# A hybrid decoder block: output projection by column halves, pooling and gate evacuated by ScalarE, first MLP sums on GpSimd

## The chip, the cores and the metric

The kernel runs on one core of a Trainium2 chip. The metric is the device time of one execution in microseconds (us). Three runs of the kernel before took 1162.57 to 1164.47 us, median 1163.44. In the profile PE is TensorE (matmul), DVE is VectorE, ACT is ScalarE, POOL is GpSimd and SP is SyncE, which issues most DMAs here.

## The reference

One decoder layer over a sequence of 1024 tokens with 1024 channels, all in float32:

```
h    = rms_norm(x, norm1_g)
proj = h @ w_in           # 8 heads x 64: q, k, v | 8 gate logits | conv input 512 | pool input 256
att  = forgetting attention: q, k normalised per head, causal, with the running sum of
       log_sigmoid(gate + b_f) as a bias, in blocks of 128 queries
conv = GLU -> causal depthwise conv of width 31 -> LayerNorm -> SiLU -> 256x256 matmul
pool = (trailing mean over 2, 4, 8, 16 tokens - self) -> 64x64 matmul per group -> scale
x    = x + concat(att, conv, pool) @ w_out          # 1024 -> 1024
h2   = rms_norm(x, norm2_g)
up   = causal depthwise conv of width 3 over h2 @ w_up     # 1024 -> 2 x 2816
out  = x + (silu(gate half of up) * value half of up) @ w_down
```

## The kernel before

**Arithmetic.** Every large product is made of three matmuls in a fast 32-bit format: each operand is split into a rounded high part and a low part (`split`, L47 to L49: ACT casts the high part, DVE or, where `lo` says so, POOL subtracts it from the source), and `mm3` (L51 to L55) issues high x high (L53), high x low (L54) and low x high (L55). A weight is ready for L53 when ACT has cast it and for L54 or L55 when the low part is there too.

**Order of the work.** The code is written for a tile framework. Its build-time scheduler puts the instructions of each engine in one fixed order and inserts the waits; each engine then runs its queue strictly in that order, so one instruction that waits holds up all behind it. The code says what depends on what, and, by generators that are advanced with `step` or `next`, what is offered to the scheduler early.

**Stage 1, to about 233 us: input projection.** x and `w_in` are loaded; eight 128-row pieces of x, transposed, are the operands `hh` and `hl` (k = 0 to 7). `feat_mm` makes the convolution and pooling inputs with channels on partitions, in two halves of 512 tokens. `feat_evac` takes each result from PSUM, times the token's 1/rms (`rb`): for kind "b" into `u` and through a sigmoid, for kind "a" into `ar` and on POOL times `u`, and in the branch under `else` into `pu`. That branch belongs to the test for "a" alone, so kind "b" runs it too and writes values into `pu` that the kind "p" overwrites later: eight products in all, L190. Then `values_in` makes v in token tiles of 128 (256 columns, in the second call 264, of which 8 are the gate logits: ACT evacuates v, DVE the gates, L422), and `heads_in` q and k. Weights come through `load_two` (two k at a time) and `load_wide` (one k, 512 columns), over two buffers named `wr`; a `wr` is free when both halves have been read.

Beside this runs the generator `side_work`: the 31 taps of the convolution over two channel groups and two halves (124 operations of 128x512 on DVE, L262 and L266, one accumulator `acc` each), and between the two channel groups the pooling chain `pool_work`: shifted adds `pn` (L234), the window's mean minus self into `d` (L245), a corrected first 16 columns copied into `d` (L247), the split of `d` into `dhl`, and a product `tp` on PE, evacuated into `mcp` (L254). After the values, `gate_cumsum` (L364 on) turns the gate logits `fgt` into log-sigmoids `fz` by ACT's Exp and Ln with DVE steps between, and sums them along the tokens.

**Stage 2, to about 430 us: attention.** 32 stages, eight heads times four blocks of 256 queries: `scores` (PE `s`, ACT exponential, DVE and POOL for the split), transposes `t`, `values`. Into these stages a second generator, `fill`, puts tiles of the output projection that need only the convolution and pooling half of the input: one tile is 12 matmuls into a bank `f`, for token tile t and one half of the output columns (L611 to L624). `mix_work` does tokens 0 to 511 for column half 0, waits until the last q and k are prepared (`prep_done`, from stage 23), then does the other three parts. A fill is offered from stage 4 on in every second stage, and in every stage once `prep_done` is set. The sums are kept in four tiles `x2`, each with two token tiles over all columns.

**Stage 3, to about 510 us.** `mix_att` adds the attention half of the output projection (banks `c`) to `x2`. `h2T` (L731 to L762) writes a token tile to DRAM by a DMA that POOL issues, takes its sum of squares on ACT and 1/rms on POOL (`ss`), scales it on DVE (`xh`, L738), transposes it on PE (`d`) and splits it into the four quadrants that the MLP needs. The MLP is a seven-product (Strassen) scheme; of the first block of `w_up`, `add_sums(0)` makes the four sums `ws` of quadrants on DVE (L712 to L719), called after token tile 3.

**Stage 4 and 5, to the end:** 22 blocks of the up-projection with the width-3 convolution and the gate, then the down-projection. The diff touches neither.

Of the kernel before, what the change touches and what calls it, by code (L numbers as in the profile page):

```python
# [16 lines left out]
P = 128  # L17
# [4 lines left out]
H = 8  # L22
# [17 lines left out]
def tile_hybrid_block(ctx: ExitStack, tc: tile.TileContext, x: bass.AP, xT: bass.AP, prm: bass.AP,  # L40
# [6 lines left out]
    def split(dst_hi, dst_lo, src, lo=None):  # L47
        nc.scalar.copy(out=dst_hi, in_=src)  # L48
        (lo or nc.vector).tensor_tensor(out=dst_lo, in0=src, in1=dst_hi.bitcast(F32), op=ALU.subtract)  # L49
# [62 lines left out]
    def tpps():  # L112
        return ptp.tile([P, 512], F32, name="tp", tag="tp")
# [63 lines left out]
    def feat_evac(pss, f, half):  # L177
        kind, i = f
        sl = slice(half * 512, half * 512 + 512)
        if kind == "b":  # L180
            ub = u[:, i, PAD + half * 512:PAD + half * 512 + 512]
            nc.vector.tensor_tensor(out=ub, in0=pss, in1=rb[:, sl], op=ALU.mult)
            nc.scalar.activation(out=ub, in_=ub, func=AF.Sigmoid)
        if kind == "a":
            ua = u[:, i, PAD + half * 512:PAD + half * 512 + 512]
            ar = raw((P, 512), "ar")
            nc.vector.tensor_tensor(out=ar, in0=pss, in1=rb[:, sl], op=ALU.mult)
            nc.gpsimd.tensor_tensor(out=ua, in0=ar, in1=ua, op=ALU.mult)
        else:
            nc.vector.tensor_tensor(out=pu[i][:, 16 + half * 512:528 + half * 512], in0=pss, in1=rb[:, sl],  # L190
                                    op=ALU.mult)

# [22 lines left out]
    def pool_work():  # L215
# [10 lines left out]
        for i in range(2):  # L226
# [22 lines left out]
            for half in range(2):  # L249
                dhl = sp.tile([P, 2, 512], F32R, name="dhl", tag="shl")  # L250
                split(dhl[:, 0], dhl[:, 1], d[:, half * 512:half * 512 + 512])
                ps = tpps()
                mm3(ps, pw_hl[:, 0, i, :], pw_hl[:, 1, i, :], dhl[:, 0], dhl[:, 1], True, True)
                nc.vector.tensor_scalar(out=mcp[half][:, 2 + i, :], in0=ps, scalar1=pc(PC_PS + i), scalar2=None,  # L254
                                        op0=ALU.mult)
                yield
# [107 lines left out]
    def gate_cumsum():  # L364
        fz = sp.tile([P, NT * H], F32, name="fz", bufs=1)
        z = fgt.rearrange("p t h -> p (t h)")
        nc.vector.scalar_tensor_tensor(out=fz, in0=z, scalar=-1.0, in1=z, op0=ALU.mult, op1=ALU.max)
# [45 lines left out]
    def values_in(c0, w, n, then, steps):  # L413
        for t in range(NT):
# [6 lines left out]
            if w > 256:  # L421
                nc.vector.scalar_tensor_tensor(out=fgt[:, t, :], in0=ps[:, 256:264], scalar=rstd[:, t:t + 1],  # L422
                                               in1=par[:, PC_BF:PC_BF + H], op0=ALU.mult, op1=ALU.add)
            step(steps)
# [44 lines left out]
    for k in range(4, KT):  # L469
        load_wide(0, k, nc.gpsimd)  # L470
    gate_cumsum()
# [105 lines left out]
    def load_wo(half, k0, pool, bufs=2):  # L577
        sl = slice(half * 512, half * 512 + 512)
        for a in range(2):
            t = s8.tile([P, 2112], F32R, name="wo", tag="s8")[:, 0:2048].rearrange("p (k a n) -> p k a n", k=2, a=2)  # L580
            for b in range(2):
# [4 lines left out]
                wo[k, half] = t[:, b]  # L586

    def x2_slice(t, half):
        return x2[t // 2][:, (t % 2) * D + half * 512:(t % 2) * D + half * 512 + 512]

# [18 lines left out]
    def mix_work():  # L609
        x2[0] = mxb.tile([P, 2048], F32, name="x2", tag="mx")  # L610
        x2[1] = mxb.tile([P, 2048], F32, name="x2", tag="mx")  # L611
        load_wo(0, 4, bp)
        yield from mix_out(0, 0)
        while not prep_done[0]:
            yield
        load_wo(1, 4, bp)
        yield from mix_out(0, 1)
        x2[2] = mxa.tile([P, 2048], F32, name="x2", tag="mx")
        x2[3] = s8.tile([P, 2112], F32, name="x2s", tag="s8")[:, 0:2048]
        yield from mix_out(1, 0)  # L620
        load_wo(0, 0, bp)
        yield from mix_out(1, 1)
# [9 lines left out]
    for n, (h, g) in enumerate(stages):  # L632
# [10 lines left out]
        values(h, g)  # L643
        if n >= 4 and (n % 2 == 0 or prep_done[0]):
            next(fill, None)
# [32 lines left out]
    hq.update({q: hx(f"h{q}") for q in ("2", "3")})  # L678
    T["22"] = (slot(s8, "s8", "t22h", F32R), slot(mxa, "mx", "t22l", F32R))

# [26 lines left out]

    def sub(out, a, b):
        nc.vector.tensor_tensor(out=out, in0=a, in1=b, op=ALU.subtract)  # L709

    ws = {}

    def add_sums(f, s):
        r = raws[f]
        ws[f] = s
        nc.vector.tensor_tensor(out=s[:, 0], in0=r[:, 3], in1=r[:, 2], op=ALU.add)
        sub(s[:, 1], s[:, 0], r[:, 0])
        sub(s[:, 2], r[:, 0], r[:, 3])
        sub(s[:, 3], r[:, 1], s[:, 1])  # L719

# [10 lines left out]
    def h2T(t):  # L731
        xh = cp.tile([P, D], F32, name="xh")
        xs = x2[t // 2][:, (t % 2) * D:(t % 2) * D + D]
        nc.gpsimd.dma_start(out=x2d[t], in_=xs)
        ss = cp.tile([P, 1], F32, name="ss2")
        nc.scalar.activation(out=xh, in_=xs, func=AF.Square, accum_out=ss)
        rsqrt(ss, ss, D, 1)
        nc.vector.scalar_tensor_tensor(out=xh, in0=xs, scalar=ss, in1=g2b, op0=ALU.mult, op1=ALU.mult)  # L738
        ts = slice((t % 4) * P, (t % 4) * P + P)
# [27 lines left out]
    for t in range(NT):  # L767
# [12 lines left out]
        h2T(t)  # L780
        if t == 3:
            split_raw(0)
            add_sums(0, slot(mxb, "mx", "ws"))
    pcx.close()
# [285 lines left out]
```

## Time and profile before

| | us |
|---|---|
| median of three runs | 1163.44 (1162.57 to 1164.47) |
| the profiled execution | 1160.78 |
| its span | 1158.8 |
| PE busy, 5476 matmuls | 1099.7 (95%) |
| DVE busy | 890.7 (77%) |
| ACT busy | 528.3 (46%) |
| POOL busy | 330.8 (29%) |
| mean granted clock of TensorE | 0.979 |

The profile shows one execution. A row of its timeline gives start, duration, engine, line, operation and tiles, and in brackets how long the engine stood idle before it and what released it. Neighbouring operations of one engine overlap a little at their ends, so a time from start to start can be shorter than one duration. PE's matmuls are pipelined; their durations say less than their starts.

### The profile page before, as it was taken

The page shows a single profiled execution, that of the slowest core. Times are in us where ns is not written, and L with a number is a line of the kernel's source. Part 1 is how long each engine was busy: PE and PEld are TensorE (multiplying, and loading weights), DVE is VectorE, ACT ScalarE, POOL GpSimd, SP SyncE. Part 2 cuts the span into 40 slices and gives each one's busy share as a digit, 9 for nine tenths or more (in the row PEclk, how much of TensorE's full clock was granted, in tenths as well). Part 3 has the DMA queues.
Part 4 walks back from the last instruction along what each step waited for, and adds up shares of the span by engine and source line. Part 5 has one row for each costly group of instructions (what it writes and reads, how often), then busy time and mean ns, then how long its engine had stood idle before and what let it go on. Part 6 is the DMA issues. An engine that isn't in the chain of part 4 may idle for free.

```text
span 1158.8 us, 14691 instructions
## 1 busy us (share of the span) xinstructions
PE 1099.7 (95%) x5476; PEld 911.0 (79%) x5476; DVE 890.7 (77%) x1275; ACT 528.3 (46%) x761; POOL 330.8 (29%) x317
## 2 busy tenths in 40 slices
PE   8989899989999989879999999999999999899997
PEld 6879778977878878758888888888888788688875
DVE  5899977568898656787877888787878755998673
ACT  7222123267897654455443535353535443233321
POOL 1252358666666641101212121212121210000010
PEclk9999999989999999979999999999999999999999
DMA  9130011043222131211213121312121397672362
GB/s 357 55 95 20 18 38 55 2 120 99 70 83 84 58 128 73 110 37 55 103 62 109 55 109 55 109 55 98 66 109 55 127 328 263 235 264 91 127 230 79
DMA packets 52727, 124.15 MB, mean 107 GB/s; under 512 B 6184, under 2 KB 11688, under 8 KB 49840
## 3 DMA queue, kind: packets, MB, share of 16 engines
q1 hardware_dynamic: 47056, 103.29, 26.7%
q0 software_dynamic: 5600, 19.93, 4.3%
q8 instruction: 43, 0.70, 0.2%
q14 instruction: 28, 0.23, 0.1%
HBM read 99.04 MB, written 19.96 MB: 103 GB/s over the span
## 4 chain that ended last, share of the span: by engine, by line
PE 68%; DVE 10%; issue 8%; DMA 7%; POOL 3%; ACT 2%; SPq 1%; POOLq 0%; DVEq 0%; ACTq 0%
PE b L53 12%; PE b L55 12%; PE b L54 12%; PE mm L53 4%; PE mm L54 4%; PE mm L55 3%; DMA dr<-gd 3%; DVE dl L49 2%; POOL w L49 2%; PE s L531 2%; DVE p L536 2%; PE c L53 1%; PE c L55 1%; PE c L54 1%; PE t L555 1%
## 5 line engine op out<-in xcount | busy, mean ns | idle before, releaser
L846 POOL TENSOR_TENSOR ac<-ac 128x1024 f32<-128x1024 f32 x22 | 61.5, 2794 | 366.8 <-ACT u L827 223.8
L802 DVE SCALAR_TENSOR_TENSOR ac<-u,par,ac 128x1023 f32<-128x1023 f32 x88 | 112.7, 1280 | 9.7 <-ACT ac L800 8.7
L53 PE MATMUL mm<-w,hh 128*128 128x256 f32 (+2 forms) x320 | 99.4, 312 | 6.9 <-DVE pu L190 3.5
L54 PE MATMUL mm<-w,hh 128*128 128x256 f32 (+2 forms) x320 | 99.3, 311 | 4.2 <-POOL w L49 4.2
L48 ACT CAST wsh<-ws 128x2048 fp32r<-128x2048 f32 x22 | 42.1, 1912 | 125.3 <-PE b L54 125.2
L55 PE MATMUL mm<-w,hl 128*128 128x256 f32 (+2 forms) x320 | 99.1, 311 | 0.0
L266 DVE SCALAR_TENSOR_TENSOR acc<-u,par,acc 128x512 f32<-128x512 f32 x120 | 97.3, 854 | 0.0
L49 DVE TENSOR_TENSOR dl<-dr,dh 128x1024 fp32r<-128x1024 f32 (+1 forms) x39 | 65.7, 1685 | 29.3 <-ACT dh L48 27.9
L543 POOL TENSOR_TENSOR p<-p,l 128x896 f32<-128x896 f32 (+3 forms) x64 | 72.8, 1152 | 38.8 <-DVE l L542 38.2
L48 ACT CAST dh<-dr 128x1024 fp32r<-128x1024 f32 (+1 forms) x39 | 54.7, 1402 | 59.4 <-PE y L55 24.7
L54 PE MATMUL x<-dl,dh 128*128 128x512 f32 x176 | 69.9, 397 | 2.2 <-DVE dl L49 2.2
L53 PEld LDWEIGHTS mm<-w,hh 128*128 128x128 f32 x320 | 61.7, 193 | 11.1 <-issue 2.8
L55 PE MATMUL x<-dh,dl 128*128 128x512 f32 x176 | 69.7, 396 | 0.0
L54 PEld LDWEIGHTS mm<-w,hh 128*128 128x128 f32 x320 | 62.1, 194 | 8.2 <-POOL w L49 5.0
L896 POOL DMA_DIRECT2D out_dram<-acc x16 | 8.7, 542 | 207.5 <-DVE acc L892 206.9
L800 ACT ACTIVATE ac<-u,par 128x1024 f32<-128x1024 f32 x44 | 50.7, 1153 | 34.3 <-DVE u L837 33.7
L49 POOL TENSOR_TENSOR w<-wr,w 128x512 fp32r<-128x512 f32 (+1 forms) x24 | 47.9, 2002 | 59.2 <-ACT w L48 59.0
L55 PEld LDWEIGHTS mm<-w,hl 128*128 128x128 f32 x320 | 62.0, 194 | 3.1
L48 ACT CAST dh<-res 128x1024 fp32r<-128x1024 f32 x22 | 23.2, 1052 | 84.2 <-PE y L55 46.3
L49 DVE TENSOR_TENSOR wsl<-ws,wsh 128x2048 fp32r<-128x2048 f32 x22 | 50.4, 2291 | 13.4 <-ACT wsh L48 13.4
L53 PE MATMUL x<-dh 128*128 128x512 f32 x176 | 53.7, 401 | 6.7 <-DVE acc L892 6.0
L709 DVE TENSOR_TENSOR ws<-wur 128x512 f32<-128x512 f32 x22 | 59.1, 2688 | 0.0
(301 smaller groups left out, 3310.5 us busy)
## 6 DMA issues: line engine op xcount, KB each, us to landing
wur<-in_w_up_dram SPq DMA_DIRECT2D x22, 1024.0 KB, 4.8
dr<-in_w_down_dram SPq DMA_DIRECT2D x66, 256.0 KB, 4.6
dr<-gd SPq DMA_DIRECT2D x55, 256.0 KB, 4.3
gd<-ac POOLq DMA_DIRECT2D x22, 512.0 KB, 3.0
wr<-in_w_in_dram SPq DMA_DIRECT2D x32, 256.0 KB, 2.7
res<-gd SPq DMA_DIRECT2D x22, 256.0 KB, 5.6
v<-in_x_dram SPq DMA_DIRECT2D x8, 512.0 KB, 8.9
ck<-cumd SPq DMA_DIRECT2D x8, 512.0 KB, 3.7
```

The lines of the kernel that those rows point to most:

```text
L48: nc.scalar.copy(out=dst_hi, in_=src)
L49: (lo or nc.vector).tensor_tensor(out=dst_lo, in0=src, in1=dst_hi.bitcast(F32), op=ALU.subtract)
L53: nc.tensor.matmul(ps, a_hi, b_hi, start=first, stop=False, skip_group_check=more)
L54: nc.tensor.matmul(ps, a_hi, b_lo, start=False, stop=False, skip_group_check=more)
L55: nc.tensor.matmul(ps, a_lo, b_hi, start=False, stop=last, skip_group_check=more)
L266: nc.vector.scalar_tensor_tensor(out=a, in0=u[:, c, o + j:o + j + 512], scalar=pc(PC_DW + c * CW + j), in1=a, op0=ALU.mult, op1=ALU.add)
L531: nc.tensor.matmul(ps[:, 0:c1 - c0], qT[:, i * P:(i + 1) * P], part[:, c0:c1], start=b == 0, stop=b == 1 and c1 < n)
L543: nc.gpsimd.tensor_tensor(out=pt[:, 0:n], in0=pt[:, 0:n], in1=l[:, 1:2].broadcast_to([P, n]), op=ALU.mult)
L709: nc.vector.tensor_tensor(out=out, in0=a, in1=b, op=ALU.subtract)
L800: nc.scalar.activation(out=ac, in_=us, func=AF.Copy, scale=pc(w0 + 2))
L802: nc.vector.scalar_tensor_tensor(out=ac[:, j:S], in0=us[:, 0:S - j], scalar=pc(w0 + 2 - j), in1=ac[:, j:S], op0=ALU.mult, op1=ALU.add)
L846: nc.gpsimd.tensor_tensor(out=a[:, 1], in0=a[:, 1], in1=a[:, 0], op=ALU.mult)
```

## The change

Six edits:

1. `feat_evac`: in the `else` branch ACT copies the bank into `pu`, and POOL multiplies `pu` by `rb` in place. This holds for kinds "b" and "p", so eight copies and eight products.
2. `pool_work`: a `yield` between the split of `d` and the matmuls on it.
3. `values_in`: ACT evacuates the gate logits, scaled by 1/rms; the bias `b_f` is added for all tiles at once in `gate_cumsum`, on DVE.
4. The low halves of input weights 4 and 6 of the first q block are made by DVE, those of 5 and 7 still by POOL.
5. `mix_work` does column half 0 for all tokens first, then waits for `prep_done`, then column half 1. For the first four token tiles `x2` is kept by column half, so that two of the four `x2` tiles are taken from other pools and at another time; `h2T` then works on these tiles in two halves (two DMAs, two sums of squares that POOL adds, two scalings). A fill is offered in every second stage up to stage 28 and in every stage after it; before, in every stage from 23 on.
6. `add_sums(0)` runs on POOL and is called after token tile 5. The slots of `T["22"]` are taken after token tile 3.

```diff
-            nc.vector.tensor_tensor(out=pu[i][:, 16 + half * 512:528 + half * 512], in0=pss, in1=rb[:, sl],
-                                    op=ALU.mult)
+            up = pu[i][:, 16 + half * 512:528 + half * 512]
+            nc.scalar.copy(out=up, in_=pss)
+            nc.gpsimd.tensor_tensor(out=up, in0=up, in1=rb[:, sl], op=ALU.mult)
...
                 split(dhl[:, 0], dhl[:, 1], d[:, half * 512:half * 512 + 512])
+                yield
...
         fz = sp.tile([P, NT * H], F32, name="fz", bufs=1)
+        nc.vector.tensor_tensor(out=fgt, in0=fgt, in1=par[:, None, PC_BF:PC_BF + H].broadcast_to([P, NT, H]),
+                                op=ALU.add)
...
-                nc.vector.scalar_tensor_tensor(out=fgt[:, t, :], in0=ps[:, 256:264], scalar=rstd[:, t:t + 1],
-                                               in1=par[:, PC_BF:PC_BF + H], op0=ALU.mult, op1=ALU.add)
+                nc.scalar.activation(out=fgt[:, t, :], in_=ps[:, 256:264], func=AF.Copy, scale=rstd[:, t:t + 1])
...
     for k in range(4, KT):
-        load_wide(0, k, nc.gpsimd)
+        load_wide(0, k, (nc.vector, nc.gpsimd)[k % 2])
...
     def x2_slice(t, half):
+        if t < 4:
+            return x2[half][:, t * 512:t * 512 + 512]
...
     def mix_work():
         x2[0] = mxb.tile([P, 2048], F32, name="x2", tag="mx")
-        x2[1] = mxb.tile([P, 2048], F32, name="x2", tag="mx")
         load_wo(0, 4, bp)
         yield from mix_out(0, 0)
+        x2[2] = mxb.tile([P, 2048], F32, name="x2", tag="mx")
+        x2[3] = s8.tile([P, 2112], F32, name="x2s", tag="s8")[:, 0:2048]
+        yield from mix_out(1, 0)
         while not prep_done[0]:
             yield
         load_wo(1, 4, bp)
+        x2[1] = s8.tile([P, 2112], F32, name="x2s", tag="s8")[:, 0:2048]
         yield from mix_out(0, 1)
-        x2[2] = mxa.tile([P, 2048], F32, name="x2", tag="mx")
-        x2[3] = s8.tile([P, 2112], F32, name="x2s", tag="s8")[:, 0:2048]
-        yield from mix_out(1, 0)
         load_wo(0, 0, bp)
         yield from mix_out(1, 1)
...
-        if n >= 4 and (n % 2 == 0 or prep_done[0]):
+        if n >= 4 and (n % 2 == 0 or n > 28):
             next(fill, None)
...
     def h2T(t):
...
+        if t < 4:
+            for half in range(2):
+                xs, sl = x2_slice(t, half), slice(half * 512, half * 512 + 512)
+                nc.gpsimd.dma_start(out=x2d[t, :, sl], in_=xs)
+                nc.scalar.activation(out=xh[:, sl], in_=xs, func=AF.Square, accum_out=ss[:, half:half + 1])
+            nc.gpsimd.tensor_tensor(out=ss[:, 0:1], in0=ss[:, 0:1], in1=ss[:, 1:2], op=ALU.add)
...
         if t == 3:
+            T["22"] = (slot(s8, "s8", "t22h", F32R), slot(mxa, "mx", "t22l", F32R))
             split_raw(0)
-            add_sums(0, slot(mxb, "mx", "ws"))
+        if t == 5:
+            add_sums(0, slot(mxb, "mx", "ws"), nc.gpsimd)
```

**POOL in the first stage** (`w` low halves of weights, `u` and `pu` evacuations; from the statistics `rstd` of the tokens to the first q statistics `ss`). Before:

```order
L188 TENSOR_TENSOR u<-ar,u 128x512 x2
L49 TENSOR_TENSOR w<-wr,w 128x2x256
L188 TENSOR_TENSOR u<-ar,u 128x512
L49 TENSOR_TENSOR w<-wr,w 128x2x256 x2
L188 TENSOR_TENSOR u<-ar,u 128x512
L49 TENSOR_TENSOR w<-wr,w 128x2x256 x5
L49 TENSOR_TENSOR w<-wr,w 128x2x264 x4
L49 TENSOR_TENSOR w<-wr,w 128x512 x8
```

Now, the later part of the same stretch:

```order
L188 TENSOR_TENSOR u<-ar,u 128x512
L49 TENSOR_TENSOR w<-wr,w 128x2x256 x4
L192 TENSOR_TENSOR pu<-pu,rb 128x512
L49 TENSOR_TENSOR w<-wr,w 128x2x256
L192 TENSOR_TENSOR pu<-pu,rb 128x512 x2
L49 TENSOR_TENSOR w<-wr,w 128x2x264 x2
L192 TENSOR_TENSOR pu<-pu,rb 128x512
L49 TENSOR_TENSOR w<-wr,w 128x2x264 x2
L49 TENSOR_TENSOR w<-wr,w 128x512 x6
```

Four products `pu` (kind "p") stand between the low halves, which were neighbours; the other four (kind "b") stand ahead of this piece, around the first two `u`. The last group has six low halves instead of eight.

**PE at the first pooling projection** (`tp<-dhl`; the `mm` around it are a token tile of v, in the order k = 0 to 7, where hh_114 and hl_122 are k = 0 and hh_119 and hl_127 are k = 5). Before:

```order
L53 MATMUL mm<-w,hh_119 128x256
L54 MATMUL mm<-w,hh_119 128x256
L55 MATMUL mm<-w,hl_127 128x256
L53 MATMUL tp<-dhl,pw_hl 128x512
L53 MATMUL mm<-w,hh_120 128x256
L54 MATMUL mm<-w,hh_120 128x256
```

Now:

```order
L53 MATMUL mm<-w,hh_114 128x256
L54 MATMUL mm<-w,hh_114 128x256
L55 MATMUL mm<-w,hl_122 128x256
L53 MATMUL mm<-w,hh_115 128x256
L54 MATMUL mm<-w,hh_115 128x256
L53 MATMUL tp<-dhl,pw_hl 128x512
L55 MATMUL mm<-w,hl_123 128x256
```

The projection moved from behind 18 matmuls of this token tile to behind 5. On DVE, counted from the first tap, the copy `d<-m` that it needs stood behind 49 taps and stands behind 52.

**DVE where q begins** (`acc` taps, `fgt` gates, `fz` the log-sigmoid, `mcp` the evacuated pooling projection of the second channel group). Before:

```order
L254 TENSOR_SCALAR mcp_131<-tp,par 128x512
L266 SCALAR_TENSOR_TENSOR acc<-u,par,acc 128x512 x2
L422 SCALAR_TENSOR_TENSOR fgt<-mm,rstd,par 128x8
L266 SCALAR_TENSOR_TENSOR acc<-u,par,acc 128x512 x2
L422 SCALAR_TENSOR_TENSOR fgt<-mm,rstd,par 128x8
L266 SCALAR_TENSOR_TENSOR acc<-u,par,acc 128x512 x4
L367 SCALAR_TENSOR_TENSOR fz<-fgt 128x64
```

Now:

```order
L256 TENSOR_SCALAR mcp_131<-tp,par 128x512
L268 SCALAR_TENSOR_TENSOR acc<-u,par,acc 128x512 x6
L49 TENSOR_TENSOR w<-wr,w 128x512
L268 SCALAR_TENSOR_TENSOR acc<-u,par,acc 128x512 x3
L368 TENSOR_TENSOR fgt<-fgt,par 128x64
L268 SCALAR_TENSOR_TENSOR acc<-u,par,acc 128x512 x2
L49 TENSOR_TENSOR w<-wr,w 128x512
L268 SCALAR_TENSOR_TENSOR acc<-u,par,acc 128x512 x2
L371 SCALAR_TENSOR_TENSOR fz<-fgt 128x64
```

The gate evacuations are gone from DVE; the low halves of weights 4 and 6 and the one bias add have come in ahead of `fz`. From the copy `d<-m` of the first channel group there are 39 taps to `fz` before, and 36 to the first of these low halves now.

More of the change, by code (lines that the diff above doesn't have):

```diff
@@ L678, in tile_hybrid_block @@
     hq.update({q: hx(f"h{q}") for q in ("2", "3")})
-    T["22"] = (slot(s8, "s8", "t22h", F32R), slot(mxa, "mx", "t22l", F32R))
     g2b = cp.tile([P, D], F32, name="g2b", bufs=1)
@@ L706, in split_raw, with sub, add_sums @@
         hl[f] = [(hi, lo)]
-    def sub(out, a, b):
-        nc.vector.tensor_tensor(out=out, in0=a, in1=b, op=ALU.subtract)
+    def sub(out, a, b, eng=nc.vector):
+        eng.tensor_tensor(out=out, in0=a, in1=b, op=ALU.subtract)
     ws = {}
-    def add_sums(f, s):
+    def add_sums(f, s, eng=nc.vector):
         r = raws[f]
         ws[f] = s
[L716 to L719, printed above, removed]
+        eng.tensor_tensor(out=s[:, 0], in0=r[:, 3], in1=r[:, 2], op=ALU.add)
+        sub(s[:, 1], s[:, 0], r[:, 0], eng)
+        sub(s[:, 2], r[:, 0], r[:, 3], eng)
+        sub(s[:, 3], r[:, 1], s[:, 1], eng)
     def prod(ps, side, i, q, first, last):
@@ L732, in h2T @@
         xh = cp.tile([P, D], F32, name="xh")
[L733 to L738, printed above, removed]
+        ss = cp.tile([P, 2], F32, name="ss2")
+        if t < 4:
[4 more added lines that the diff above has]
+            nc.gpsimd.tensor_tensor(out=ss[:, 0:1], in0=ss[:, 0:1], in1=ss[:, 1:2], op=ALU.add)
+        else:
+            xs = x2[t // 2][:, (t % 2) * D:(t % 2) * D + D]
+            nc.gpsimd.dma_start(out=x2d[t], in_=xs)
+            nc.scalar.activation(out=xh, in_=xs, func=AF.Square, accum_out=ss[:, 0:1])
+        rsqrt(ss[:, 0:1], ss[:, 0:1], D, 1)
+        for half in range(2 if t < 4 else 0):
+            sl = slice(half * 512, half * 512 + 512)
+            nc.vector.scalar_tensor_tensor(out=xh[:, sl], in0=x2_slice(t, half), scalar=ss[:, 0:1], in1=g2b[:, sl],
+                                           op0=ALU.mult, op1=ALU.mult)
+        if t >= 4:
+            nc.vector.scalar_tensor_tensor(out=xh, in0=xs, scalar=ss[:, 0:1], in1=g2b, op0=ALU.mult, op1=ALU.mult)
         ts = slice((t % 4) * P, (t % 4) * P + P)
```

## The prediction

> **What bounds the kernel now.** I read the page's first two parts, then the waits of PE, then the busy time by stage, then single rows around each wait.
>
> ```profile
> span 1158.8 us, 14691 instructions
> PE 1099.7 (95%) x5476; PEld 911.0 (79%) x5476; DVE 890.7 (77%) x1275; ACT 528.3 (46%) x761; POOL 330.8 (29%) x317
> PE   8989899989999989879999999999999999899997
> DVE  5899977568898656787877888787878755998673
> ```
>
> PE sets the time almost everywhere: it is busy for 95% of the span. A change that removes no matmuls can only win what PE loses to waits, to issue and to a lowered clock, some tens of us at most. The waits say where.
>
> ```profile
> PE b L53 <- ACT t1h L48: 5.0, 1, 5.0
> PE mm L54 <- POOL w L49: 4.2, 1, 4.2
> PE s L531 <- DVE m L536: 4.1, 9, 1.1
> PE mm L53 <- DVE pu L190: 3.5, 2, 2.5
> PE t L555 <- DVE pt L49: 2.5, 5, 1.0
> PE mm L53 <- DVE fgt L422: 2.3, 1, 2.3
> PE tp L53 <- ACT dhl L48: 1.9, 1, 1.9
> ```
>
> Columns: total us, times, longest. Four rows belong to the first stage and name what the diff touches: the pooling evacuation (3.5), the gate evacuation (2.3), the pooling projection that waits for `dhl` (1.9) and the low half of an input weight on POOL (4.2), 11.9 us together. Two (`s`, `t`: 6.6 us in 14 waits) lie in attention. `t1h` (5.0) ends the h2T stage. The busy time by stage (busy us per engine with instruction counts, then PE's granted clock):
>
> ```profile
> 80.00:100.00 20.00, 17.54 (x138) 17.34 (x138) 19.95 (x30) 2.91 (x6) 1.39 (x1) 0.91 0.10 29
> 100.00:120.00 20.00, 17.60 (x140) 16.94 (x138) 19.97 (x26) 6.63 (x13) 9.17 (x4) 1.00 0.19 54
> 120.00:140.00 20.00, 18.19 (x118) 17.31 (x119) 20.00 (x40) 4.20 (x9) 4.76 (x1) 0.91 0.00 1
> 140.00:160.00 20.00, 15.80 (x63) 11.94 (x62) 12.69 (x22) 5.59 (x8) 12.56 (x6) 0.91 0.20 54
> 480.00:520.00 40.00, 28.21 (x114) 21.65 (x113) 33.80 (x40) 18.04 (x24) 2.71 (x6) 0.79 0.15 53
> ```
>
> From 80 to 140 us the third column, DVE, is full. PE waits there because DVE, which runs 124 convolution taps, reaches each small job late. So in this stage the question isn't which engine evacuates a bank, but when DVE comes to the next thing that PE needs. Waits of 2 us and more also leave a window at clock 0.91.
>
> **The change, part by part.**
>
> *1. Pooling evacuation.* Eight DVE products go; eight ACT copies and eight POOL products in SBUF come. PE's bank is then freed by ACT, 2.91 us busy of 20 there: the 3.5 us of waits on `pu` go. DVE's price for the POOL products shows where POOL already works beside the taps:
>
> ```profile
> 40.25 0.68 DVE L190 TENSOR_TENSOR pu<-s,rb 128x512 f32<-128x512 f32 x1
> 40.85 0.68 DVE L182 TENSOR_TENSOR u<-s,rb 128x512 f32<-128x512 f32 x1
> 139.87 2.73 DVE L266 SCALAR_TENSOR_TENSOR acc<-u,par,acc 128x512 f32<-128x512 f32 x4
> L266 DVE SCALAR_TENSOR_TENSOR acc<-u,par,acc 128x512 f32<-128x512 f32 x25 | 29.1, 1214 | 0.0
> L49 POOL TENSOR_TENSOR w<-wr,w 128x512 fp32r<-128x512 f32 x8 | 12.3, 1543 | 9.5 <-ACT w L48 9.5
> L49 POOL TENSOR_TENSOR w<-wr,w 128x528 fp32r<-128x528 f32 x4 | 6.2, 1551 | 3.8 <-ACT w L48 3.8
> L188 POOL TENSOR_TENSOR u<-ar,u 128x512 f32<-128x512 f32 x2 | 3.1, 1542 | 3.0 <-DVE ar L187 3.0
> 42.87 2.14 POOL L188 TENSOR_TENSOR u<-ar,u 128x512 f32<-128x512 f32 x2 [13.97 <-DVE ar L187]
> ```
>
> A product starts 0.60 us after the one before it: eight save 4.8 us. Four quiet taps take 2.73 us, 0.68 each (0.74 as one duration). In the window 50 to 82 us (the four grouped rows) 25 taps average 1.214 us beside 14 POOL operations: (1.214 - 0.74) x 25 / 14 = 0.85 us of DVE per POOL operation. Eight new ones cost 6.8 us; from 0, if they fall beside products that read PSUM (as the last row's two, 1.07 us each, did), to 8.6, if each blocks DVE for a full 1.07. I take 6.8, since taps are most of what DVE runs there. The change may cost DVE more than it saves.
>
> The Trainium skill (SBUF — State Buffer, "Who interferes with whom") says that a DVE instruction with two SBUF inputs and a GpSimd instruction that reads SBUF contend, and that the later one blocks fully rather than being slowed. The trace agrees in kind: 0.85 us of 1.07. By that rule the price would be the upper end, 1.8 us more than the sum takes.
>
> *2. The yield.* It lets the scheduler put the first pooling projection earlier on PE: after 5 matmuls of a token tile instead of 18, so 13 matmuls earlier. On DVE, the copy that completes `d` now stands behind 52 taps instead of 49.
>
> ```profile
> 101.85 0.15 DVE L247 COPY d<-m 128x16 f32<-128x16 f32 x1
> 102.71 0.50 PE L53 MATMUL tp<-dhl,pw_hl 128*128 128x512 f32 x1 [1.90 <-ACT dhl L48]
> 142.52 0.22 DVE L367 SCALAR_TENSOR_TENSOR fz<-fgt 128x64 f32<-128x64 f32 x1
> 142.65 2.73 DVE L266 SCALAR_TENSOR_TENSOR acc<-u,par,acc 128x512 f32<-128x512 f32 x4
> 146.56 0.50 PE L54 MATMUL mm<-w,hh 128*128 128x512 f32 x1 [4.20 <-POOL w L49]
> ```
>
> DVE finishes `d` at 101.85 - 4.8 + 3 x 0.68 + 6.8 = 105.9, and PE starts `tp` 0.86 later, at 106.7 (99.9 without the POOL price, 108.5 at 1.07). PE has then done 13 matmuls fewer than before at 102.71. At 17.60 us for 140 they are 1.6 us: PE is 4.0 + 1.6 = 5.6 us behind. Several short waits have become one long one: PE would be there at 102.71 - 1.90 - 3.5 - 1.6, less 1.6 of clock (9% of 17.54), so at 94.1, and stands for 12.6 us. Such a stall costs clock afterwards: 9% of 15.80 us = 1.4 behind the 4.2 us wait, 21% of 28.21 = 5.9 where PE idles 11.8 us of 40 in pieces. I take 2.5, nearer to the single wait. PE is 8.1 us behind.
>
> The Trainium skill (TensorE: Matmul & The Clock Gate, "Why this matters for your kernels") has one idle window of a little over 3 us bring the array back to half clock. By it, this one stall would cost a window at half speed, an estimate of 1.7 us, and the sum would be 0.8 us better.
>
> *3. Gate evacuation by ACT.* The 2.3 us wait for `fgt` goes, and with it the clock of 120 to 140 (9% of 18.19 = 1.6): PE is 8.1 - 3.9 = 4.2 us behind. One small add joins DVE.
>
> *4. Low halves of weights 4 and 6 on DVE, 5 and 7 on POOL.* Before, DVE took 142.52 - 101.85 = 40.7 us from `d` to `fz` over 39 taps. Now 36 taps stand between `d` and the low half of weight 4, and eight gate operations are gone, each 0.13 from its start to the next one's, as `fz` took (142.52 to 142.65): 40.7 - 2.0 - 1.0 = 37.7. That half is ready at 105.9 + 37.7 + 0.7 = 144.3. PE would be there at 146.56 - 4.20 + 4.2 = 146.6. No wait; the clock loss of 1.4 behind the old one goes. **First stage: 1.4 us faster.** The end without POOL price gives 6.8 more (8.2); at 1.07 it is 0.4 slower.
>
> *5. Output projection by column halves.* All four tiles of (1,0) run during stages 12 to 18 of attention, where before nothing was filled in; the later fills thin out, 6 tiles instead of 9 in stages 23 to 31.
>
> ```profile
> 300.00:360.00 60.00, 57.87 (x388) 46.96 (x387) 55.68 (x164) 55.13 (x121) 41.17 (x35) 1.00 0.32 89
> 360.00:410.00 50.00, 49.02 (x313) 41.70 (x311) 34.11 (x99) 34.73 (x75) 35.65 (x30) 1.00 0.21 71
> ```
>
> Until 360 DVE and ACT are over 90% busy and PE idles; behind it they have room (68%), so thinning can cost little. The 6.6 us of waits lie over 32 stages. Four fills cover about eight of these: 6.6 x 8/32 = 1.6, of which I take **1.6 us faster** (ends: 2 slower, if the thinned part waits; 6 faster, if nearly all waits go).
>
> *6. h2T and the first sums.*
>
> ```profile
> 463.62 0.68 DVE L716 TENSOR_TENSOR ws<-wur 128x512 f32<-128x512 f32 x1
> 473.92 1.28 DVE L738 SCALAR_TENSOR_TENSOR xh<-x,ss,g2b 128x1024 f32<-128x1024 f32 x1 [1.28 <-POOL ss L84]
> 491.78 0.68 DVE L49 TENSOR_TENSOR t22l<-d,t22h 128x512 fp32r<-128x512 f32 x1
> 504.27 0.68 DVE L49 TENSOR_TENSOR t1l<-h,t1h 128x512 fp32r<-128x512 f32 x1
> ```
>
> DVE loses four sums of 0.60; POOL gains them around the statistics of tiles 4 and 5, which they delay by up to 1.55 each, so 3 us for a tile. The chain that ends the stage, from the last `xh` to `t1l` at 504.27, is tile 7's and keeps its operations. I cost this at nothing: the statistics of tiles 6 and 7 come later in POOL's queue than the sums. If that cover fails, it costs 3 us. The halved DMAs and statistics of tiles 0 to 3 add one POOL DMA and one small add each. From 520 on, nothing changes.
>
> **The sum:** 1.4 + 1.6 = 3.0 us. The profiled execution took 1160.8 us (span 1158.8), 2.7 below the median of 1163.4; set against the median, the forecast is 1163.4 - 3.0 = **1160.4**.
>
> **The rivals.**
>
> *A, slower: POOL starves on weight 5.* A POOL operation that starts while DVE runs taps can be held up instead of holding DVE up.
>
> ```profile
> 105.63 6.11 POOL L49 TENSOR_TENSOR w<-wr,w 128x512 fp32r<-128x512 f32 x2 [22.81 <-ACT w L48]
> 135.24 12.51 POOL L49 TENSOR_TENSOR w<-wr,w 128x512 fp32r<-128x512 f32 x2 [18.75 <-ACT w L48]
> 152.70 0.20 DVE L369 TENSOR_SCALAR fz<-fz 128x64 f32<-128x64 f32 x1 [7.31 <-ACT fz L368]
> ```
>
> Two pairs that began after some 20 us without POOL work took 6.11 and 12.51 us, where two took 2.14 above. The second ended only once DVE ran dry, at 152.70 - 7.31 = 145.4. Now weight 5's low half is the first after such a pause. Its cast comes with PE 4.2 us later, at about 139 to 140. If nothing lets POOL in, DVE runs on to the `fz` operation that waits for ACT's exponential, eleven taps, weight 6's half and two small operations behind 144.3 (7.5 + 0.7 + 0.3), near 153. PE needs the half at 146.6 plus weight 4's six matmuls of 512 columns (1.4 us), 148. It waits 5 us, some 2 more for weight 7, which waits for the same buffers, and 1.5 of clock: 8.5 us over the forecast, 1168.9. It decides once the operation takes over 8 us. For it: two cases of two. Against: DVE has to wait for weight 6's cast too, an opening near 148, and then the cost is 0 to 2. Chance 0.27.
>
> *B, faster: the POOL products find gaps.* Then `d` is ready at 99.1, and the first stage brings 8.2 us: 1153.6. For: four of the eight are due near 42 us, beside DVE's PSUM products. Against: 25 taps at 1.214. Chance 0.12.
>
> *C, no difference: the fills give nothing.* The thinned stages wait as much as the early ones gain, or a little more (up to 2): 1162.0 to 1164.0. The POOL price of 1.07 alone ends there too, at 1162.2. For: the waits there are of many kinds, none longer than 1.1 us. Against: DVE and ACT have room behind 360. Chance 0.15.
>
> *D, no difference to slightly slower: the sums on POOL delay tile 6 as well.* For: the row of 473.92 shows DVE waiting 1.28 us for such a statistic. Against: the sums are due with tiles 4 and 5. It gives 3 us back: 1163.4, with clock 1165. Chance 0.12.
>
> **How the numbers follow.** About 0.2% (2.3 us) can be told from no change, so faster means below 1161.1, slower above 1165.8. The forecast has 0.34, its own range 1156 to 1163: 0.25 faster, 0.09 same. A: 0.02, 0.04, 0.21. B: 0.12 faster. C: 0.02, 0.10, 0.03. D: 0.02, 0.05, 0.05. Sums: 0.43, 0.28, 0.29. The range reaches from B short of its best third, 1152, to A at its price, 1169.
>
> **What would show it.** Right: no waits on `pu` and `fgt`; one wait of 9 to 13 us at `tp` for `dhl`, with `d` near 106; more slowed taps than before ahead of it; PE at weight 4 near 146.6 without a wait on it. In attention, waits of `s` and `t` near 5 us. Wrong: `d` before 102 (B); a POOL `w` of over 8 us near 140 to 153 with PE behind it (A); more PE idle from 360 to 410 than 2 us (C); PE waiting for `xh` of tile 6 (D).

## The result, and the profile after

The changed kernel takes 1172.92 us in the median of five runs (1169.32 to 1175.07), the kernel before 1162.57 us beside it (1159.76 to 1164.47): **0.84% slower**, ratio 1.0084 with an interval of 1.0059 to 1.011. The forecast was 1160.4 us, 3.0 us faster, with a range up to 1169. The profiled execution of the changed kernel has a span of 1170.7 us, 11.9 more than before.

First PE's waits in the changed kernel (total us, times, longest):

```profile
PE tp L53 <- ACT dhl L48: 13.1, 1, 13.1
...
PE mm L53 <- DVE qk L460: 3.8, 2, 3.4
PE tp L53 <- ACT s__1624 L48: 3.0, 1, 3.0
...
PE mm L55 <- POOL w L49: 1.1, 1, 1.1
PE mm L53 <- ACT w L48: 1.1, 1, 1.1
```

The waits on `pu` (3.5), `fgt` (2.3) and the low half of weight 4 (4.2) are gone, as the change meant it. In their place stands one wait of 13.1 us for `dhl`, a longer one for `qk` (1.1 before) and a new one for `s_`; the prediction has no word on the last two. The busy time by stage shows where they lie, first in the changed kernel, then the last two windows before:

```profile
80.00:100.00 20.00, 16.79 (x144) 16.59 (x143) 19.96 (x21) 3.46 (x8) 7.60 (x5) 1.00 0.20 54
100.00:120.00 20.00, 10.11 (x58) 9.73 (x59) 19.97 (x35) 3.71 (x7) 3.15 (x1) 0.66 0.00 1
160.00:200.00 40.00, 36.27 (x187) 29.82 (x185) 32.07 (x61) 9.43 (x16) 27.50 (x32) 1.00 0.13 34
200.00:250.00 50.00, 46.76 (x363) 45.51 (x364) 24.82 (x57) 16.92 (x30) 28.48 (x52) 0.97 0.06 18
```

```profile
160.00:200.00 40.00, 40.00 (x228) 34.57 (x226) 34.78 (x67) 9.59 (x16) 30.46 (x35) 1.00 0.15 41
200.00:250.00 50.00, 47.86 (x374) 45.02 (x372) 28.17 (x63) 21.25 (x37) 30.82 (x58) 1.00 0.13 33
```

From 100 to 120 us PE is busy for half the time, at a granted clock of 0.66. From 160 to 250 it is busy 4.8 us less than before, where none of the six edits puts an instruction.

To see what each stage costs, I take PE's lag: the time at which it starts a matmul, less what all matmuls ahead of it take at their usual distance (0.228 us for 512 columns, 0.119 for 256, 0.109 for 128, worked out from the traces). The lag grows by waits, slow starts and lowered clock alone, and it can be compared at the same amount of work done, though the order differs. It is for one execution of each kernel. In us, for the two kernels and three experiments of below:

| at this point (us of work done) | before | changed | e2 | e3 | e8 |
|---|---|---|---|---|---|
| ahead of the pooling projection (83) | 15.2 | 12.7 | 14.1 | 15.7 | 13.1 |
| behind it (92) | 17.2 | 28.5 | 20.1 | 17.9 | 28.1 |
| weight 4 of q (126) | 27.4 | 28.3 | 19.8 | 19.9 | 29.3 |
| near the end of q (160) | 28.0 | 30.0 | 22.9 | 23.6 | 32.8 |
| in k (174) | 30.0 | 38.4 | 30.8 | 25.8 | 34.8 |
| attention begins (216) | 29.6 | 38.2 | 30.6 | 25.4 | 34.3 |
| attention ends (405) | 56.1 | 62.8 | 54.7 | 49.6 | 61.7 |
| up-projection begins (440) | 73.2 | 81.5 | 72.3 | 67.0 | 80.2 |
| up-projection ends (900) | 80.0 | 88.1 | 79.0 | 73.7 | 86.9 |
| in the down-projection (1050) | 93.5 | 105.3 | 95.6 | 89.3 | 101.3 |

Executions of one order differ, so a few us between two columns are no finding by themselves: the kernel before and e3 have the same order on every engine up to about 289 us, and at 126 they are 7.5 us apart (27.4 and 19.9), most of it by the wait of 4.2 us on weight 4 and the lowered clock behind it, which e3's execution doesn't have.

In its execution the changed kernel is only 2.0 us behind the kernel before at 160, loses 6.4 more up to 174 (8.4 where before lost 2.0), wins 1.9 in attention (24.6 where before lost 26.5), loses 1.6 in the h2T stage and 3.7 in the down-projection.

**What DVE paid.** DVE in the changed kernel: eleven taps in a row, the copy that completes `d`, and the taps of the stretch from 50 to 92 us as a group, with POOL's groups there:

```profile
78.00 13.75 DVE L268 SCALAR_TENSOR_TENSOR acc<-u,par,acc 128x512 f32<-128x512 f32 x11
109.03 0.16 DVE L248 COPY d<-m 128x16 f32<-128x16 f32 x1
L268 DVE SCALAR_TENSOR_TENSOR acc<-u,par,acc 128x512 f32<-128x512 f32 x31 | 39.3, 1326 | 0.0
L49 POOL TENSOR_TENSOR w<-wr,w 128x512 fp32r<-128x512 f32 x8 | 13.1, 1652 | 3.0 <-ACT w L48 3.0
L192 POOL TENSOR_TENSOR pu<-pu,rb 128x512 f32<-128x512 f32 x4 | 6.7, 1683 | 0.0
```

The eleven taps take 1.25 us on average (13.75 / 11), where a quiet one takes 0.68. Singly, the six that run beside POOL's work take 1.78 to 1.82 each, and the five behind it 0.74. `d` is complete at 109.03, 3.1 us later than forecast and 7.2 later than before.

**What happened near 200 us.** PE, POOL, DVE and ACT of the changed kernel at the waits for `qk` and `s_`, row by row from the timeline:

```profile
194.25 1.65 POOL L84 TENSOR_TENSOR ss<-ss,nhalf 128x8 f32<-128x8 f32 x1
195.86 1.29 POOL L49 TENSOR_TENSOR w<-wr,w 128x512 fp32r<-128x512 f32 x1
...
197.79 1.26 POOL L49 TENSOR_TENSOR w<-wr,w 128x512 fp32r<-128x512 f32 x1
199.03 0.32 POOL L458 TENSOR_SCALAR ss<-ss,rstd 128x8 f32<-128x8 f32 x1
199.38 0.76 DVE L460 TENSOR_TENSOR qk<-mm,ss 128x256 f32<-128x256 f32 x2 [1.83 <-POOL ss L458]
200.28 0.36 PE L53 MATMUL mm<-w,hh 128*128 128x256 f32 x1 [3.41 <-DVE qk L460]
205.41 1.28 ACT L295 ACT_TABLE_LOAD   x1
208.05 0.61 ACT L48 CAST s__1624<-sf 128x512 fp32r<-128x512 f32 x1
208.71 0.73 PE L53 MATMUL tp<-s__1624,cw_hl 128*128 128x512 f32 x2 [2.96 <-ACT s__1624 L48]
```

PE waits for a bank that DVE evacuates into `qk`; DVE waits for the statistic `ss`; and on POOL two low halves of weights (`w`) stand between the two operations that make this statistic (`L84` and `L458`). They are weights for k columns that PE needs later. Then PE, in its fixed order, is sent to the convolution's pointwise product while ACT is still loading the table for SiLU. Before, there was one low half between the two operations, and PE had 2.9 us of other matmuls ahead of the product:

```profile
191.95 2.19 POOL L84 TENSOR_TENSOR ss<-ss,nhalf 128x8 f32<-128x8 f32 x1
194.49 1.30 POOL L49 TENSOR_TENSOR w<-wr,w 128x512 fp32r<-128x512 f32 x1 [0.35 <-ACT w L48]
195.78 0.32 POOL L455 TENSOR_SCALAR ss<-ss,rstd 128x8 f32<-128x8 f32 x1
196.12 0.76 DVE L457 TENSOR_TENSOR qk<-mm,ss 128x256 f32<-128x256 f32 x2 [1.54 <-POOL ss L455]
```

From the start of the one operation to the start of the other it takes 4.8 us now (194.25 to 199.03) and took 3.8 before (191.95 to 195.78). So POOL's queue explains about 1 us of the difference between the two kernels here; the rest of the wait of 3.4 us is that PE, in its new order, comes to this bank earlier against the statistic.

### The profile page after: what moved, and what is told of

The parts are those of the page before. It is cut to its first block, busy times and chain, and to the rows that moved or that the text cites. A ratio compares the mean times of both kernels' runs of the same rounds, so it can differ in the third digit from the quotient of the medians.

```text
span 1170.7 us, 14708 instructions
## 1 busy us (share of the span) xinstructions
PE 1099.4 (94%) x5476; PEld 912.8 (78%) x5476; DVE 896.1 (77%) x1262; ACT 534.4 (46%) x785; POOL 342.3 (29%) x335
## 3 DMA queue, kind: packets, MB, share of 16 engines
HBM read 99.04 MB, written 19.96 MB: 102 GB/s over the span
## 4 chain that ended last, share of the span: by engine, by line
PE 58%; DVE 16%; issue 15%; DMA 5%; ACT 2%; POOL 2%; SPq 1%; POOLq 0%; DVEq 0%; ACTq 0%
PE b L55 12%; PE b L53 12%; PE b L54 12%; DVE acc L268 8%; PE s L534 2%; PE t L558 2%; DMA xr<-in_xT_dram 1%; PE f L53 1%; PE mm L53 1%; PE mm L54 1%; PE f L55 1%; PE c L53 1%; PE mm L55 1%; PE px L567 1%; PE f L54 1%
## 5 line engine op out<-in xcount | busy, mean ns | idle before, releaser
L268 DVE SCALAR_TENSOR_TENSOR acc<-u,par,acc 128x512 f32<-128x512 f32 x120 | 105.9, 935 | 0.0
L48 ACT CAST dh<-dr 128x1024 fp32r<-128x1024 f32 (+1 forms) x39 | 54.6, 1401 | 58.5 <-PE y L55 24.6
L49 DVE TENSOR_TENSOR pt<-t,pt 128x512 fp32r<-128x512 f32 (+1 forms) x80 | 49.5, 631 | 12.5 <-ACT pt L48 12.2
```

Of the source, the lines that this page charges most:

```text
L268: nc.vector.scalar_tensor_tensor(out=a, in0=u[:, c, o + j:o + j + 512], scalar=pc(PC_DW + c * CW + j), in1=a, op0=ALU.mult, op1=ALU.add)
```

## The experiments

All are timed in five rounds beside the kernel before, and ratios are to that. The median, the ratio and its interval:

| | us | ratio | interval |
|---|---|---|---|
| changed kernel | 1172.92 | 1.0084 | 1.0059 to 1.011 |
| e1, edit 1 alone | 1174.61 | 1.0111 | 1.0079 to 1.0143 |
| e2, without edit 1 | 1165.58 | 1.0044 | 1.002 to 1.0068 |
| e3, edits 5 and 6 alone | 1157.29 | 0.9977 | 0.9953 to 1.0 |
| e4, product on DVE | 1165.66 | 1.003 | 1.0007 to 1.0053 |
| e5, conv tail later | 1178.98 | 1.0158 | 1.0125 to 1.019 |
| e6, projection later | 1172.43 | 1.0102 | 1.0073 to 1.0131 |
| e7, lean, conv tail later | 1171.91 | 1.01 | 1.007 to 1.0131 |
| e8, last weights on DVE | 1167.72 | 1.0046 | 1.0027 to 1.0066 |
| e9, edits 5 and 6, last weights on DVE | 1169.37 | 1.006 | 1.004 to 1.0079 |
| e10, as e9, without the useless products | 1158.22 | 0.9966 | 0.9947 to 0.9986 |
| e11, e8 without edit 1 | 1159.48 | 0.9969 | 0.9946 to 0.9992 |
| e12, e11 without the useless products | 1158.27 | 0.9958 | 0.9938 to 0.9977 |

**e1: edit 1 alone.** To the kernel before, only this:

```diff
+            up = pu[i][:, 16 + half * 512:528 + half * 512]
+            nc.scalar.copy(out=up, in_=pss)
+            nc.gpsimd.tensor_tensor(out=up, in0=up, in1=rb[:, sl], op=ALU.mult)
```

> The kernel before with edit 1 alone (ACT copies the pooling banks, POOL multiplies). Theory E1 (edit 1 makes the loss, by DVE's slowed taps and by the order that the scheduler then gives PE): 7 to 11 us slower than before, PE waits over 10 us at tp for dhl, and again 5 to 7 us around 200 us at mm for qk and at tp for s_. Theory BACK (the loss of the first stage is won back in attention; the column halves and the sums on POOL make the rest): 2 to 5 us slower. Theory GATE (the gate and the weight halves make it): within 2 us of before.

It is 1.1% slower, more than the whole change and a little more than theory E1 named (7 to 11 us). PE's waits in it:

```profile
PE tp L53 <- ACT dhl L48: 13.4, 2, 13.2
...
PE mm L53 <- DVE qk L458: 6.2, 3, 4.6
...
PE tp L53 <- ACT s__1623 L48: 3.0, 1, 3.0
```

All three waits come with edit 1. It also corrects the prediction's account of the order: this kernel has no yield, and its first pooling projection stands on PE behind the same 5 matmuls of the token tile as in the changed kernel. The kernel before with the yield alone has the old order on every engine, and e2, which has the yield and not edit 1, has PE's old order up to about 126 us. So edit 1 moved the first projection, and not the yield. A likely reason, not traced, is that the scheduler, with DVE rid of the products, expects `d` earlier and doesn't count what POOL's products cost DVE.

**e2: the changed kernel without edit 1.** `feat_evac` as before, all else as changed.

> The changed kernel with edit 1 undone (DVE evacuates the pooling banks as before). Theory E1: 1 to 5 us faster than before; the waits of 1.0 and 2.5 us on pu are back, the wait at tp for dhl is near 2 us, and around 200 us PE loses no more than before. Theory BACK: 3 to 6 us slower than before. Theory GATE: 6 to 10 us slower.

0.44% slower than before: theory E1 doesn't hold alone. Its waits:

```profile
PE mm L53 <- DVE qk L459: 6.0, 3, 2.4
...
PE tp L53 <- ACT dhl L48: 3.0, 1, 3.0
```

The long wait is gone, and at 160 us of work this kernel is as far as e3 (lag 22.9 and 23.6). But from 160 to 174 it loses 7.9 us, and e3 only 2.2. So the loss near 200 us needs neither edit 1 nor DVE's lateness from it: it comes with edits 2 to 4 too, and those put no instruction there.

**e3: edits 5 and 6 alone.** The first stage has the old order on every engine.

> The kernel before with edits 5 and 6 alone (column halves, h2T in halves, first sums on POOL). Theory E1: 1 to 3 us faster than before (attention wins about 2 us as in the trace of the change, the h2T stage gives up to 2 back). Theory BACK: 3 to 6 us slower. The first stage has the same order as before on every engine, so it shows nothing of edits 1 to 4.

Faster by 0.23%, with an interval that ends at 1.0, so a gain is likely and not quite shown. From 216 to 405 the lag grows by 24.2 us, 2.3 less than before. Theory BACK, which had this kernel slower, falls: edits 5 and 6 are not the loss. It comes with edits 1 to 4, which all act in the first stage.

**e4: the eight products on DVE.** To the changed kernel:

```diff
-            nc.gpsimd.tensor_tensor(out=up, in0=up, in1=rb[:, sl], op=ALU.mult)
+            nc.vector.tensor_tensor(out=up, in0=up, in1=rb[:, sl], op=ALU.mult)
```

> The changed kernel, but DVE and not POOL makes the eight products in SBUF after ACT's copies: DVE has the eight operations of 0.6 us back and loses the contention. Theory E1: no loss, 0 to 4 us faster than before, the d copy near 102 to 104 us instead of 109. If the ACT copies were the trouble and not the products on POOL: 6 us or more slower than before.

The copy into `d` in this kernel:

```profile
105.30 0.16 DVE L248 COPY d<-m 128x16 f32<-128x16 f32 x1
```

DVE does all eight products itself and still has `d` 3.7 us earlier than with POOL's help. The ratio falls from 1.0084 to 1.003, about where e2 is, which has neither ACT's copies nor POOL's products. ACT's copies are not the trouble. The ranges named (`d` near 102 to 104, the kernel 0 to 4 us faster than before) were missed. PE still waits 8.7 us for `dhl` here, then 5.1 us in one piece for `qk` just ahead of 166 us, and near 200 us two more waits for `qk` cost it 2.7 us.

**e5: the convolution's tail at a lower priority.** To the changed kernel:

```diff
-        yield from conv_tail(0)
-        yield from conv_tail(1)
+        for half in range(2):
+            gen = conv_tail(half)
+            while True:
+                with tc.high_priority(offset=-80):
+                    done = next(gen, 0) == 0
+                if done:
+                    break
+                yield
```

> The changed kernel with the instructions of the convolution's tail (transposes, statistics, SiLU, pointwise product) offered to the scheduler at a lower priority; up to about 155 us every engine has the order of the changed kernel. On PE the first pointwise matmul now stands some 4 us of matmuls behind the transposes that feed it, instead of directly behind them. Theory TAIL (the loss of the changed kernel arises where PE is sent to that product before ACT has made its input): PE loses about 2 us around 200 to 212 us instead of 8, and the kernel is 4 to 7 us faster than the changed one, within 0.5% of before. Theory DHL (the 13 us wait for dhl is the loss): the wait stays, and the kernel stays 8 to 12 us slower than before.

Slower, 1.6%: a miss. PE's waits:

```profile
PE mm L53 <- DVE qk L466: 5.2, 3, 3.3
...
PE f L408 <- DVE kl L416: 4.9, 1, 4.9
```

The wait for `s_` is gone, but those for `qk` stay, and a new one has come up where attention is prepared: PE waits for the transposed k (`kl`), ahead of which ACT now makes other casts, one of them of the tail's output. Theory TAIL had taken one of two waits of the same place for the cause.

**e6: the pooling projection later on PE.** To the changed kernel:

```diff
-                mm3(ps, pw_hl[:, 0, i, :], pw_hl[:, 1, i, :], dhl[:, 0], dhl[:, 1], True, True)
+                with tc.high_priority(offset=-400):
+                    mm3(ps, pw_hl[:, 0, i, :], pw_hl[:, 1, i, :], dhl[:, 0], dhl[:, 1], True, True)
```

> The changed kernel with the matmuls of the pooling projection alone at a lower priority: on PE they stand some 25 us of matmuls later (first channel group) and 15 us later (second), behind the time at which DVE has d ready. Theory DHL: the 13 us wait at tp goes, and the kernel becomes 8 to 13 us faster than the changed one. Theory TAIL, with DVE as the bound of the stage: the wait goes, but PE then waits about as long, 10 to 13 us in sum, further on for the next thing that DVE makes (the low half of weight 4, the q evacuation), and the time stays within 3 us of the changed kernel.

The wait of 13.1 us is gone and the time stays: 1172.43. The windows and the waits show where it went:

```profile
80.00:100.00 20.00, 20.00 (x172) 19.95 (x171) 19.96 (x20) 4.44 (x9) 9.59 (x6) 1.00 0.20 54
100.00:120.00 20.00, 13.98 (x105) 13.77 (x104) 19.97 (x31) 4.43 (x10) 6.13 (x3) 0.83 0.10 27
```

```profile
PE mm L53 <- ACT v L425: 6.0, 1, 6.0
PE tp L53 <- DVE mcp L257: 5.8, 1, 5.8
```

PE runs through 80 to 100 us without a gap and then waits 6.0 us for ACT (whose queue stands behind the cast of `d`) and 5.8 for DVE. Up to weight 4, DVE (19.96 and 19.97 of 20 us busy) sets the pace, and moving PE's work against it only moves the wait.

**e7: a lean version.** Edits 5 and 6, the useless products of kind b left out (below), and the tail's priority lowered by 120.

> The kernel before with edits 5 and 6, with kind b no longer writing into the pooling tile (four useless DVE products of 0.6 us gone, same output), and with the convolution's tail at a lower priority. Theory TAIL with DVE as the bound: 2.4 us of DVE's first stage go and the tail costs no more than before: 1 to 4 us faster than edits 5 and 6 alone (1157.3 there), 5 to 9 us faster than before. Theory DHL says nothing here but that the short wait for dhl near 2 us stays.

1% slower: a miss, as e5. Beside e3 it has only the lowered priority and four DVE products less, and e10, which leaves out the same products, is not slower than before; so the lowered priority is the likely cause. Where it loses wasn't traced.

**e8: the last four low halves on DVE.** To the changed kernel:

```diff
-    heads_in(512, 1, 256, later(load_two, 4, 768, 256, nc.gpsimd), 0)
+    heads_in(512, 1, 256, later(load_two, 4, 768, 256, None), 0)
```

> The changed kernel, but the low halves of the last four input weights (columns 768 to 1023, wanted while the last q and k tiles are evacuated) are made by DVE instead of POOL. Theory POOLQ (the loss around 190 to 212 us comes from POOL's queue, in which these halves stand between the q and k statistics, so that PE's banks come free late): the waits at mm for qk and at tp for s_ fall from 6.8 us to under 3, PE loses 2 to 4 us there instead of 8, and the kernel is 4 to 7 us faster than the changed one (1166 to 1169). Theory DVE (DVE is late by the pooling products, and everything behind it too): DVE gets four operations more, and the kernel is no faster than the changed one or up to 3 us slower.

1167.72, as theory POOLQ had it (1166 to 1169). The wait for `qk`, and the window that was at 46.76 us of PE:

```profile
PE mm L53 <- DVE qk L460: 2.1, 2, 1.7
```

```profile
200.00:250.00 50.00, 48.76 (x396) 47.77 (x397) 28.71 (x66) 18.29 (x33) 29.46 (x58) 1.00 0.09 25
```

There is no wait for `s_`, and the lag grows by 2.0 us from 160 to 174 instead of 8.4; as this execution came to 160 some 2.8 us later, it is 3.9 us ahead of the changed kernel's at 216. Up to about 196 us both have the same order on every engine. So the loss near 200 us lies in the order behind that, and goes when these low halves leave POOL. The edit also moves operations on the other engines there, and the runs don't separate the two. What is left (0.46%) comes mostly from the first stage up to weight 4: the wait of 13.2 us is in this kernel as in the changed one.

**e9: the same on top of edits 5 and 6.**

> The kernel before with edits 5 and 6 and the last four low halves on DVE. There PE loses only 2 us around 190 to 205 us. Theory POOLQ: 0 to 2 us faster than edits 5 and 6 alone (1157.3 there). Theory DVE: up to 3 us slower than these.

A miss: 0.6% slower than before. PE's waits in it, and the POOL operation for weight 4 in it and in e3, whose first stage has the same order up to there:

```profile
PE s L531 <- DMA ck<-cumd: 5.3, 1, 5.3
PE mm L54 <- POOL w L49: 4.2, 1, 4.2
```

```profile
136.88 11.30 POOL L49 TENSOR_TENSOR w<-wr,w 128x512 fp32r<-128x512 f32 x1 [18.73 <-ACT w L48]
```

```profile
134.07 3.23 POOL L49 TENSOR_TENSOR w<-wr,w 128x512 fp32r<-128x512 f32 x2 [16.29 <-ACT w L48]
```

Two things stand in this profile that e3's doesn't have. The new order has the last transposes of q and k directly ahead of the first scores, which then wait for a DMA (5.3 us). In e8, e10, e11 and e12 some 3 us of work stand between. So the same edit can lose by its order what it wins in POOL's queue. And POOL's half of weight 4 took 11.30 us here, where in e3 it and the next one took 3.23 together. This is not the edit's doing: up to about 189 us e9, e3 and the kernel before have the same order on every engine, and in the profile of the kernel before the two took 12.51. Whether POOL gets in between DVE's taps differs from execution to execution.

**e10: the useless products left out as well.**

```diff
-        else:
+        elif kind == "p":
```

> As the one before, and kind b no longer writes into the pooling tile (four useless DVE products less, same output). Theory POOLQ with DVE as the bound of the first stage: another 1 to 3 us faster, 4 to 8 us faster than before. If the new order of the first stage loses it again, as edits 3 and 4 did: 2 us faster to 4 us slower than before.

0.34% faster than before, some 4 us, at the near end of what was expected; against e9 it is 11 us faster, where 1 to 3 were expected. It is not to be told from e3 (0.9977), so neither the useless products nor the last low halves show a gain on top of edits 5 and 6. That e9 is so much slower than both goes with its order ahead of the scores.

**e11 and e12: the changed kernel without edit 1, last weights on DVE; e12 without the useless products.**

> The changed kernel without edit 1 and with the last four low halves on DVE, so e8 without edit 1. Its order where attention is prepared has the same distance between the last q and k transposes and the first scores as e8. Theory BOTH (edit 1 makes the first stage itself slower, by DVE's slowed taps and the long wait with its lowered clock, and POOL's queue makes the loss around 200 us on top): the wait for dhl near 2 to 3 us, PE up to 160 us as in the version without edit 1, and 5 to 8 us faster than e8: 1158 to 1162, 0 to 4 us faster than before. Theory POOLQ ALONE (edit 1 cost nothing but the new order around 200 us): within 2 us of e8, 1166 to 1169.

> As the one before, and kind b no longer writes into the pooling tile (four DVE products of 0.6 us less, same output). Theory BOTH, with DVE as the bound of the first stage: another 0 to 2 us faster, 2 to 6 us faster than before, and with the half of weight 4 on DVE fewer runs with a wait on POOL there than in e10. Theory POOLQ ALONE: within 2 us of e8.

0.31% and 0.42% faster than before: theory BOTH. e8 and e11 differ in edit 1 alone, and in the orders that come with it; their ratios are 0.77% apart (1.0046 and 0.9969), 9 us. e2 and e11 differ in the last low halves alone, have the same order on every engine up to about 188 us, and are 0.75% apart. So each of the two losses is worth some 9 us where it is the only one. The changed kernel has both and is 1.15% slower than e11, less than the two together; that a stage which is late anyway hides part of the second is likely, not shown.

The profile of e11 doesn't show this: its execution took 1163.13 us, 3.7 above e11's median, and at 160 us of work PE is already about 9 us later than in e2's profile with the same order, with one wait of 4.2 us for `qk` and a lowered clock behind it. The expectation that PE would be there as in e2 was missed, and the second loss rests on the timed runs. e12 has the lowest ratio of the study, 0.9958 (0.9938 to 0.9977), but its interval overlaps those of e3, e10 and e11.

## Why the prediction was wrong

**The step that failed** is the end of part 4, where the first stage's sum was closed at weight 4 ("First stage: 1.4 us faster"). It failed on both sides of that point.

*Behind weight 4* the prediction put nothing, because no edit is there. But the stage goes on to attention, and from 160 to 174 PE lost 6.4 us more than before. The scheduler writes the whole order anew, and its order near 200 us has two low halves between two operations of one statistic and PE sent early to what waits for them. e2 shows the loss without edit 1; in e8 and e11 it goes with these halves off POOL (e2 and e11: 0.75%).

*Up to weight 4* the sum held within 2.3 us in the two profiles: at 126 us of work the changed kernel was 0.9 us behind, not 1.4 ahead. That is in part luck. The sum had PE 8.1 us behind after the pooling projection (11.3 in the profiles) and then took 9.5 as won back: the waits of 2.3 and 4.2 us on `fgt` and weight 4, with 1.6 and 1.4 of clock. These it read from one execution as fixed costs. e3, with the order of before, has no wait on weight 4, and against it the changed kernel is 8.4 us behind at 126. Timed, edit 1 costs 9 us where the second loss is absent (e8 and e11).

By its other steps:

- *Price of a POOL product, 0.85 us, at most 1.07:* too low. 99.1 was the forecast for `d` without them, 109.03 was measured: 9.9 us, or 1.24 for each of eight more POOL operations beside taps (seven of the products and one `u`; the first product ran beside DVE's products from PSUM). By the prediction's own reckoning the changed kernel's rows give (1.326 - 0.74) x 31 / 18 = 1.01. The Trainium skill's rule (SBUF — State Buffer, "Who interferes with whom": the later instruction blocks fully) put 1.07 on each, and was nearer than the average of rows. Single rows agree with it: from 50 to 92 us a tap that runs wholly beside POOL's work takes 1.75 to 1.83 us, one without it 0.74, about one POOL operation more. The average of 0.85 also held POOL operations that fell in part beside DVE work from PSUM. e4 shows the sign: DVE is faster doing the products itself.
- *The yield moves the projection:* wrong; edit 1 does (e1).
- *One long wait of 12.6 us at `tp`:* right, 13.11. *2.5 us of clock behind it:* right; the lag grew by 15.8 us from 83 to 92, 2.7 more than the wait. The granted clock was 0.50 from 101.8 us, inside the wait, to 115.4, which is 5.5 us past its end. The estimate by the Trainium skill's rule of one window at half speed (TensorE: Matmul & The Clock Gate, "Why this matters for your kernels") was 1.7.
- *DVE sets the pace up to weight 4, the waits only move:* right, and e6 shows it most plainly. *No wait on weight 4:* right.
- *That the old waits on weight 4 are won:* only against executions that have them; of the three profiles with this order, the kernel before and e9 have the wait of 4.2 us, and e3 has none.
- *Attention, 1.6 us faster:* not shown. It was 1.9 in the changed kernel's profile and 2.3 in e3's, but e8, with the same fills, lost 27.4 us from 216 to 405, more than the 26.5 before, and e1, without edit 5, lost some 4 us less than before. One profile each can't tell 1.6 us. PE was busy 49.96 of the 50 us from 360 to 410 in the changed kernel, so the thinner fills left no idle time there.
- *h2T at nothing:* nearly; 1.6 us slower in the changed kernel, 0.3 in e3. That is rival D's place and half its price, but not its sign: PE's longest wait for `xh` is 1.8 us in both kernels.
- *Rival A, POOL starved on weight 5:* not seen; the operation took 4.26 us and PE did not wait for it. In e11 and e12 it took 6.50 and 6.76.

What stays open: the down-projection, which no edit touches, grows the lag by 17.2 us in the changed kernel's profile, 13.5 before, 15.6 in e3 and 14.4 in e8. It was not tried what makes these differ. Why the scheduler orders POOL's queue near 200 us as it does was not traced either, nor how much of the second loss is POOL's queue and how much is the new order of the other engines.

## What to carry to other kernels

Moving work from a full VectorE to GpSimd in SBUF was no relief here, where VectorE itself reads two operands from SBUF: price the move by what the full engine loses, and try the same work on the full engine first. In a kernel whose order a build-time scheduler writes, a change is not local: compare the order of every engine to the end of the stage, and look for operations that a chain needs and that stand behind others in a strict queue. A wait that appears in one profile may be chance; compare two executions of the same order before counting it as a gain.

## What the runs showed of the hardware

Taps on VectorE (two operands from SBUF) and GpSimd operations of 128x512 slow each other. In the changed kernel, from 50 to 92 us, a tap takes 0.74 us with no GpSimd operation beside it and 1.75 to 1.83 wholly beside GpSimd work; a multiplication by `rb` on GpSimd takes 1.30 us beside VectorE products from PSUM (at 41.72 us) and 1.68 on average among the taps. The averages of 1.25 and 1.33 us for a tap mix the two kinds.

Now and then GpSimd is instead held off altogether: 11.30 us for one such operation in e9, and 12.51 for two in the kernel before, while in e3, with the same order up to there, two took 3.23.

A wait of PE of 13 us cost about 2.7 us more by the clock behind it: 0.50 was granted until 5.5 us past the end of the wait.
